# Four blocks of first products per two PSUM banks and one gelu, scores called later, left-over dots called beside the weights

## The chip, the cores and the metric

One core of a Trainium2 chip runs the kernel. The metric is the device time in microseconds (us) of one execution; the time before is the median of three runs.

## The reference, cut to what matters

The layer has two mixers (a linear recurrence and a gated linear attention) and then PEER, a channel mixer that picks experts by product keys. The change lies in PEER. For each of 512 tokens with normed vector `u` (1024 numbers), eight heads each choose 16 of 16384 experts, and the layer adds the chosen experts' outputs:

```python
q = (u @ w_q).reshape(tokens, 8 heads, 2 halves, 128)
s = einsum("thjd,hjkd->thjk", q, keys)          # 128 keys for each half
# top 16 of each half, then top 16 of the 16 x 16 sums: 16 experts per head
w = softmax(top16_scores)                       # per head
y = sum over heads and picks of  w * gelu(u . expert_u[e]) * expert_v[e]
```

## The kernel before, in words

The 512 tokens are four tiles of 128. For tiles t0 and t1 (`GT`) the kernel gathers rows of the two expert tables by an indirect DMA on the GpSimd queue (POOL): for a tile and a pick k, one gather fetches 128 rows of 4 KB (0.524 MB). For tiles d0 and d1 (`DT`) it computes all 16384 experts densely, in 128 blocks of 128 experts. A block of the first table (`ut_s`, 0.524 MB, loaded by SyncE, SP) gives the first products of both tiles, and a block of the second (`vt_s`, as large) is multiplied by the gated weights.

Four stages matter here, with their times in the profiled execution:

- **First products** (about 409 to 950 us). TensorE (PE) does 128 blocks, `d_scores` (L985 to L994): eight F32 matmuls of 128x256 per block; two blocks share one PSUM bank (`pds2`), and ScalarE (ACT) takes one gelu per bank (L994). Between the first blocks stand the eight heads' queries of the dense tiles, `q_mm` (L727, matmuls L732, copy of the result by ACT L734), and their scores, `s_mm` (L737, matmuls L742, copies L746). VectorE (DVE) picks the top 16 (`select`, L753 to L844, with an exp on ACT at L832) and, between its steps, computes dots of gathered rows of the first table (`u_row`: gather L888, dot L895), 16 at a time finished by a small gelu on ACT and a product on DVE (`u_done`, L897). `turn` (L871) transposes a dense tile's picks: DVE writes `est` (L842 and L877), PE transposes it into `ptr` (L880). `turn_i` (L902) and `turn_a` (L909) do the same for the indices (`ixf`, `pti`, `ix`) and the activations (`pta`) of t0.
- **Weights** (950 to 1142 us). 32 turns of a loop of two (L1172 to L1180): `w_hot` builds one-hot matrices `ab` on DVE and ACT, `w_mm` multiplies them on PE (`pwb`, L1015), `v_load_pairs` gathers four row groups of the second table (POOL, tiles `ring` and `ring_s`), `v_pairs` (L934) multiplies them into `yv` on PE, `w_mul` (L1024) multiplies the gelus `A` by the weights on DVE.
- **Last products** (1142 to 1550 us). 128 blocks of the second table (loop L1204 to L1221): `v_split` casts a block into a high and a low part (ACT L1037, L1038; DVE L1039, L1040), `d_out` (L1052) does 12 F32R matmuls, or 8 plain F32 ones in each sixth block. Spread over these blocks runs `rest()` (L1190): the dots of t1 that are not done yet, then its 128 row groups of the second table (`v_row`, DVE L943).
- A tail of some 19 us.

The order of the first products comes from two generators, `pe_list` (L1077) and `dve_list` (L1130), merged by planned costs (what they `yield`, and `clock` at L1154). A scheduler then orders every engine's instructions by its own estimate of times. Only the weights and the last products are pinned as written (`tc.manual_schedule`), on PE, ACT and DVE. At the end of the first products 232 of the 256 dots of gathered rows are done; 24 dots of t1 are left for `rest()`.

Of the kernel before, what the change touches and what calls it, by code (L numbers as in the profile page):

```python
# [20 lines left out]
D = 1024  # L21
# [9 lines left out]
TOPK = 16  # L31
# [16 lines left out]
def tile_kernel(ctx, tc, x, cx, pos, ada_w, cols, rows, consts, w_in, wgate, w_g, w_out, w_q, keys_t,  # L48
# [11 lines left out]
    def bank(name="ps"):  # L60
        return psum.tile([128, 512], F32, name=name, tag="ps")
# [829 lines left out]

    def u_row(t, k):
        more = "sel" not in done and k % 3 == 2
        g = gather(peer_u, sel_i[t][:, k:k + 1], zs.tile([128, D], F32, name="rz", bufs=2) if more else ring())
        V.scalar_tensor_tensor(g, g, 1.0, u_n[t], op0=OP.mult, op1=OP.mult, accum_out=act[t][:, k:k + 1])  # L895

    def u_done(t, h):  # L897
# [87 lines left out]
    def d_scores(b):  # L985
        ut = ld.pop(b)
        if b % 2 == 0:
            ld["ps"] = bank("pds2")
        p = ld["ps"][:, b % 2 * 256:b % 2 * 256 + 256]
        for k in range(KD):  # L990
            PE.matmul(p, ut[:, k], u_d[k // 4][:, k % 4].rearrange("p j t -> p (j t)"),  # L991
                      start=(k == 0), stop=(k == KD - 1))
        if b % 2:
            S.activation(a_of(b - 1, 2), ld["ps"], AF.Gelu)  # L994

# [64 lines left out]
    def u_next(t):  # L1060
# [3 lines left out]
        left[t]["u"].pop(0)  # L1064
        u_row(t, k)
        if k % TOPK == TOPK - 1:
            u_done(t, k // TOPK)
            if k == NSEL - 1 and t == t0:
                turn_a(t0)
        return True  # L1070

    def row_u():
        return u_next(t0) or (not left[t0]["u"] and u_next(t1))

    done = set()

    def pe_list():  # L1077
# [30 lines left out]
        for n, (kind, b) in enumerate(seq):  # L1108
            if n + 3 < len(seq):
                u_load(*seq[n + 3])  # L1110
            if kind == "w":
                if b % 2:
                    last = q_mm(DT, b // 2)
                    yield 7.
                continue
# [4 lines left out]
            d_scores(b)  # L1120
            if last:
                s_mm(*last)
                last = None
                yield 1.1
            yield 3.5
# [42 lines left out]
    wb = [(t, n0) for t in DT for n0 in range(0, 128, 4)]  # L1168
    with tc.manual_schedule(engines=PIN):
        gz = v_load_pairs(0, 1)  # L1170
        hot = [w_hot(*wb[n]) for n in range(2)]
        for n in range(0, 64, 2):  # L1172
# [6 lines left out]
            for q in p:  # L1179
                w_mul(*q)  # L1180
    for b in range(4):
        v_load(b)
# [7 lines left out]
    def rest():  # L1190
        for h in range(NH):
            while len(left[t1]["u"]) > NSEL - (h + 1) * TOPK:
                u_next(t1)
                yield
# [98 lines left out]
```

## Time and profile before

| | us |
|---|---|
| median of three runs | 1569.45 |
| lowest, highest | 1563.09, 1569.67 |
| profiled execution, own time | 1570.65 |
| its span in the trace | 1568.8 |
| PE busy | 1468.1 (94%) |
| DVE busy | 1191.9 (76%) |
| POOL busy | 653.5 (42%) |
| ACT busy | 533.2 (34%) |

The shares are averages over stages with different limits, so what a stage is worth must be read from that stage. Busy time of PE is what the trace models for pipelined matmuls. The profiled execution lies 1.20 us above the median. Over the span the kernel moves 484.30 MB.

### The profile page before, as it was taken

How to read it: one execution, taken by the hardware profiler on the slowest of the kernel's cores; microseconds unless marked ns; L12 is line 12 of the kernel's file. 1: busy time of each engine (PE TensorE's matmuls, PEld its weight loads, DVE VectorE, ACT ScalarE, POOL GpSimd, SP SyncE). 2: the span in 40 equal slices, each digit the busy share in tenths (PEclk: the TensorE clock that was granted, in tenths of full speed). 3: DMA queues.
4: the chain of work that ended last, by engine and by line, in shares of the span. 5: the costliest groups of instructions: out<-in, count | busy, mean ns of one | idle time of the engine just before them, and what ended most of it. 6: DMA issues, size and time to landing. Idle time of an engine off the chain costs nothing.

```text
span 1568.8 us, 20348 instructions
## 1 busy us (share of the span) xinstructions
PE 1468.1 (94%) x6668; PEld 1099.7 (70%) x6668; DVE 1191.9 (76%) x2942; ACT 533.2 (34%) x1033; POOL 653.5 (42%) x651
## 2 busy tenths in 40 slices
PE   7899999999999959998999999999979899999995
PEld 2678778468888748887888886555556676666663
DVE  5889975427999999986555545666669898988987
ACT  3657874112211211210110004455433333434333
POOL 0111100004556456475444435666535555544540
PEclk9999999999999979999999999999999999999998
DMA  9655531627899979999999998999999999999995
GB/s 372 194 185 178 160 94 54 255 85 284 309 382 331 331 259 360 346 368 351 373 377 361 389 365 279 353 354 349 345 330 367 346 393 384 379 384 363 382 369 208
DMA packets 152570, 484.30 MB, mean 309 GB/s; under 512 B 14864, under 2 KB 36752, under 8 KB 152336
## 3 DMA queue, kind: packets, MB, share of 16 engines
q0 software_dynamic: 79072, 287.87, 50.2%
q1 hardware_dynamic: 73392, 195.13, 33.5%
q8 instruction: 53, 0.87, 0.2%
q14 instruction: 53, 0.43, 0.1%
HBM read 477.69 MB, written 5.24 MB: 308 GB/s over the span
## 4 chain that ended last, share of the span: by engine, by line
PE 38%; DVE 26%; DMA 16%; issue 10%; POOL 4%; ACT 4%; DVEq 0%; POOLq 0%; ACTq 0%; SPq 0%
PE pds L991 14%; DMA ring<-in_dram,sel_i 11%; PE yv L934 7%; DVE ring L895 6%; PE pwb L1015 4%; PE pw L687 4%; POOL ring L888 3%; DVE rz L895 3%; PE ya L1052 2%; DMA rz<-in_dram,sel_i 2%; PE pq L732 1%; DVE y L943 1%; DMA wada<-in_dram 1%; DMA adw<-in_dram 1%; DVE vl L1040 1%
## 5 line engine op out<-in xcount | busy, mean ns | idle before, releaser
L888 POOL DMA_INDIRECT ring<-in_dram,sel_i x334 | 403.3, 1207 | 404.6 <-DVE ring L895 150.1
L991 PE MATMUL pds<-u_d,ut_s 128*128 128x256 f32 x2048 | 450.7, 382 | 5.0 <-DVE ix L907 5.0
L991 PEld LDWEIGHTS pds<-u_d,ut_s 128*128 128x128 f32 x2048 | 391.8, 192 | 59.1 <-DVE ix L907 5.4
L895 DVE SCALAR_TENSOR_TENSOR ring<-ring,u_n 128x1024 f32<-128x1024 f32 x206 | 255.7, 1246 | 102.1 <-DMA ring<-in_dram,sel_i 100.6
L943 DVE SCALAR_TENSOR_TENSOR y<-ring,act,y 128x1024 f32<-128x1024 f32 x127 | 162.6, 1280 | 37.2 <-DMA ring<-in_dram,sel_i 36.3
L1052 PE MATMUL ya<-vl,gh 128*128 128x512 f32 x428 | 139.3, 407 | 24.9 <-DVE vl L1040 24.6
L1052 PE MATMUL ya<-vh,gh 128*128 128x512 f32 x428 | 142.6, 415 | 2.6 <-ACT vh L1038 2.6
L1040 DVE TENSOR_TENSOR vl<-vt_s,vh 128x1024 fp32r<-128x1024 f32 x107 | 132.8, 1241 | 4.1 <-ACT vh L1038 4.1
L1052 PE MATMUL ya<-vh,gl 128*128 128x512 f32 x428 | 133.9, 394 | 0.0
L1038 ACT CAST vh<-vt_s 128x1024 fp32r<-128x1024 f32 x107 | 112.4, 1050 | 51.1 <-DMA vt_s<-in_dram 44.4
L934 PE MATMUL yv<-ring_s,z 128*64 128x512 f32 x256 | 120.5, 602 | 2.6 <-DMA ring_s<-in_dram,ix 2.5
L934 PE MATMUL yv<-ring,z 128*64 128x512 f32 x256 | 117.4, 599 | 0.0
L1052 PEld LDWEIGHTS ya<-vl,gh 128*128 128x128 f32 x428 | 78.3, 190 | 54.9 <-DVE vl L1040 39.4
L994 ACT ACTIVATE A<-pds 128x512 f32<-128x512 f32 x64 | 37.4, 596 | 225.7 <-PE pds L991 214.7
L1037 ACT CAST gh<-A 128x256 fp32r<-128x256 f32 x107 | 43.4, 406 | 191.2 <-PE ya L1052 176.8
L1000 DVE TENSOR_TENSOR ab<-cst,sel_t 128x512 f32<-128x512 f32 x64 | 44.1, 689 | 81.0 <-PE pwb L1015 50.5
L1052 PEld LDWEIGHTS ya<-vh,gh 128*128 128x128 f32 x428 | 80.7, 189 | 30.9 <-issue 9.8
L1052 PEld LDWEIGHTS ya<-vh,gl 128*128 128x128 f32 x428 | 81.0, 189 | 19.7
L888 POOL DMA_INDIRECT ring<-in_dram,ix x64 | 62.7, 980 | 50.8 <-PE yv L934 22.2
L1015 PEld LDWEIGHTS pwb<-ab 128*128 128x128 f32 x512 | 60.2, 191 | 26.4 <-issue 14.8
L1052 PE MATMUL ya<-vt_s,A 128*128 128x512 f32 x168 | 75.5, 592 | 0.0
L888 POOL DMA_INDIRECT ring_s<-in_dram,ix x64 | 61.1, 955 | 33.6 <-issue 13.5
(307 smaller groups left out, 2291.1 us busy)
## 6 DMA issues: line engine op xcount, KB each, us to landing
ut_s<-in_dram SPq DMA_DIRECT2D x144, 512.0 KB
vt_s<-in_dram SPq DMA_DIRECT2D x128, 512.0 KB
adw<-in_dram POOLq DMA_DIRECT2D x34, 512.0 KB
wraw<-in_dram SPq DMA_DIRECT2D x21, 512.0 KB
wada<-in_dram SPq DMA_DIRECT2D x16, 512.0 KB
wq<-in_dram SPq DMA_DIRECT2D x16, 512.0 KB
ring<-in_dram,sel_i POOLq DMA_INDIRECT x334
wo<-in_dram SPq DMA_DIRECT2D x8, 512.0 KB
```

The lines of the kernel that those rows point to most:

```text
L687: PE.matmul(p, mix_k(k)[:, t * 128:(t + 1) * 128], wo[k][:, n * 512:(n + 1) * 512], start=(k == 0), stop=(k == KD - 1))
L888: G.indirect_dma_start(out=g, out_offset=None, in_=tab, in_offset=bass.IndirectOffsetOnAxis(ap=ix, axis=0))
L895: V.scalar_tensor_tensor(g, g, 1.0, u_n[t], op0=OP.mult, op1=OP.mult, accum_out=act[t][:, k:k + 1])
L934: PE.matmul(yv[0][h * 64:h * 64 + 64, n, :], z[:, 63 - i:127 - i], g[:, n * 512:(n + 1) * 512], start=(i == 0), stop=(i == 63), skip_group ...
L943: V.scalar_tensor_tensor(L["y"], g, a, L["y"], op0=OP.mult, op1=OP.add)
L991: PE.matmul(p, ut[:, k], u_d[k // 4][:, k % 4].rearrange("p j t -> p (j t)"), start=(k == 0), stop=(k == KD - 1))
L1000: V.tensor_tensor(ab[:, 0], iota[:, None, :].to_broadcast([128, 4, 128]), st[0][:, j, n0:n0 + 4, None].to_broadcast([128, 4, 128]), op=OP. ...
L1015: PE.matmul(p[:, n * 128:(n + 1) * 128], ab[:, 1, n], ab[:, 0, n], start=True, stop=True)
L1037: S.copy(gh, a)
L1038: S.copy(vh, vt)
L1040: V.tensor_sub(vl, vt, vh.bitcast(F32))
L1052: PE.matmul(ya[t][:, n, :], g[:, j * 128:(j + 1) * 128], v[:, n * 512:(n + 1) * 512], start=(b == 0 and i == 0), stop=(b == 127 and i == l ...
```

## The change

Three edits. Four blocks of first products go into two neighbouring PSUM banks (`pds4`) and one gelu of 128x1024 reads them. In `pe_list` the scores of a head are called just before the queries of the next head, with a planned cost of 8.1 in place of 7 and 1.1 (the last head's after block 34). `u_row` is split into `u_start` (the gather) and `u_fin` (the dot and what follows it), and the weights loop calls them from its second turn on: the dot of the row that was started one turn earlier, then the gather of the next, into a tile `rw` that reuses the two buffers of `u_d`. `rest()` keeps what is then left.

```diff
--- before.py
+++ after.py
@@ -889,10 +889,21 @@
                              in_offset=bass.IndirectOffsetOnAxis(ap=ix, axis=0))
         return g
 
-    def u_row(t, k):
-        more = "sel" not in done and k % 3 == 2
-        g = gather(peer_u, sel_i[t][:, k:k + 1], zs.tile([128, D], F32, name="rz", bufs=2) if more else ring())
+    def u_start(t, k):
+        if "u" in done:
+            g = B.tile([128, D], F32, name="rw", tag="u_d", bufs=2)
+        elif "sel" not in done and k % 3 == 2:
+            g = zs.tile([128, D], F32, name="rz", bufs=2)
+        else:
+            g = ring()
+        return t, k, gather(peer_u, sel_i[t][:, k:k + 1], g)
+
+    def u_fin(t, k, g):
         V.scalar_tensor_tensor(g, g, 1.0, u_n[t], op0=OP.mult, op1=OP.mult, accum_out=act[t][:, k:k + 1])
+        if k % TOPK == TOPK - 1:
+            u_done(t, k // TOPK)
+            if k == NSEL - 1 and t == t0:
+                turn_a(t0)
 
     def u_done(t, h):
         a = act[t][:, h * TOPK:(h + 1) * TOPK]
@@ -984,14 +995,14 @@
 
     def d_scores(b):
         ut = ld.pop(b)
-        if b % 2 == 0:
-            ld["ps"] = bank("pds2")
-        p = ld["ps"][:, b % 2 * 256:b % 2 * 256 + 256]
+        if b % 4 == 0:
+            ld["ps"] = bank2("pds4")
+        p = ld["ps"][:, b % 4 // 2, b % 2 * 256:b % 2 * 256 + 256]
         for k in range(KD):
             PE.matmul(p, ut[:, k], u_d[k // 4][:, k % 4].rearrange("p j t -> p (j t)"),
                       start=(k == 0), stop=(k == KD - 1))
-        if b % 2:
-            S.activation(a_of(b - 1, 2), ld["ps"], AF.Gelu)
+        if b % 4 == 3:
+            S.activation(a_of(b - 3, 4), ld["ps"].rearrange("p h n -> p (h n)"), AF.Gelu)
 
     def w_hot(t, n0):
         j = DT.index(t)
@@ -1062,15 +1073,13 @@
         if k >= NSEL or k >= ready_h[t] * TOPK:
             return False
         left[t]["u"].pop(0)
-        u_row(t, k)
-        if k % TOPK == TOPK - 1:
-            u_done(t, k // TOPK)
-            if k == NSEL - 1 and t == t0:
-                turn_a(t0)
-        return True
+        return u_start(t, k)
 
     def row_u():
-        return u_next(t0) or (not left[t0]["u"] and u_next(t1))
+        g = u_next(t0) or (not left[t0]["u"] and u_next(t1))
+        if g:
+            u_fin(*g)
+        return g
 
     done = set()
 
@@ -1110,18 +1119,19 @@
                 u_load(*seq[n + 3])
             if kind == "w":
                 if b % 2:
+                    if last:
+                        s_mm(*last)
                     last = q_mm(DT, b // 2)
-                    yield 7.
+                    yield 8.1
                 continue
             if b == A1:
                 while "sel" not in done:
                     yield None
                 open_l2()
             d_scores(b)
-            if last:
+            if last and b == 34:
                 s_mm(*last)
                 last = None
-                yield 1.1
             yield 3.5
             if b == 121:
                 done.add("end")
@@ -1167,6 +1177,7 @@
     PIN = {ET.Activation, ET.PE, ET.DVE}
     wb = [(t, n0) for t in DT for n0 in range(0, 128, 4)]
     with tc.manual_schedule(engines=PIN):
+        late = []
         gz = v_load_pairs(0, 1)
         hot = [w_hot(*wb[n]) for n in range(2)]
         for n in range(0, 64, 2):
@@ -1178,6 +1189,12 @@
             gz = gzn
             for q in p:
                 w_mul(*q)
+            if 2 <= n:
+                if late:
+                    u_fin(*late.pop())
+                g = n < 56 and u_next(t1)
+                if g:
+                    late.append(g)
     for b in range(4):
         v_load(b)
     if "usage" in globals():
@@ -1190,7 +1207,7 @@
     def rest():
         for h in range(NH):
             while len(left[t1]["u"]) > NSEL - (h + 1) * TOPK:
-                u_next(t1)
+                u_fin(*u_next(t1))
                 yield
             for _ in range(TOPK):
                 v_row(t1, left[t1]["v"].pop(0))
```

The order in which each engine receives its instructions, at three places. First ACT among the first products, where the dense heads' queries are copied (`q`), the exponentials of a selection are taken (`sw`), scores are copied (`s`) and gelus of first products go to `A1`. Before:

```order
L994 ACTIVATE A1_3042<-pds2_3925 128x512
L832 ACT_TABLE_LOAD
L832 ACTIVATE sw_4497<-sw_4497 128x64
L734 COPY q_3998<-pq_3981 128x512
L899 ACT_TABLE_LOAD
L899 ACTIVATE act0_2314<-act0_2314 128x16
L746 COPY s_3751<-pss_4045 128x256
L746 COPY s_3753<-pss_4045 128x256
L994 ACTIVATE A1_3042<-pds2_4036 128x512
```

and in the changed kernel:

```order
L1005 ACTIVATE A1_3042<-pds4_3772 128x1024
L734 COPY q_3985<-pq_3968 128x512
L832 ACT_TABLE_LOAD
L832 ACTIVATE sw_4475<-sw_4475 128x64
L910 ACT_TABLE_LOAD
L910 ACTIVATE act0_2314<-act0_2314 128x16
L746 COPY s_3817<-pss_4108 128x256
L746 COPY s_3819<-pss_4108 128x256
L1005 ACTIVATE A1_3042<-pds4_3906 128x1024
```

The copy of the queries stood behind the exponential and now stands ahead of it.

Second PE, where the picks of d0 are transposed (`ptr`). Before (63 blocks of first products stand ahead of `ptr`):

```order
L991 MATMUL pds_4858<-u_d,ut_s 128x256 x16
L991 MATMUL pds_4903<-u_d,ut_s 128x256 x8
L906 MATMUL pti<-cst,ixf 128x128
L880 MATMUL ptr<-cst,est 128x128 x3
L991 MATMUL pds_4903<-u_d,ut_s 128x256 x8
L991 MATMUL pds_4965<-u_d,ut_s 128x256 x16
```

and in the changed kernel, from the last head's scores on (31 blocks stand ahead of `pti`, 43 ahead of `ptr`):

```order
L742 MATMUL pss<-kt,q 128x128 x4
L917 MATMUL pti<-cst,ixf 128x128
L1002 MATMUL pds_4068<-u_d,ut_s 128x256 x8
L1002 MATMUL pds_4204<-u_d,ut_s 128x256 x32
L1002 MATMUL pds_4290<-u_d,ut_s 128x256 x32
L1002 MATMUL pds_4393<-u_d,ut_s 128x256 x24
L880 MATMUL ptr<-cst,est 128x128 x3
L1002 MATMUL pds_4393<-u_d,ut_s 128x256 x8
```

`ptr` moved 20 blocks nearer to the start, and eight matmuls stand for one block. In both kernels the scores of a dense head still stand about one block behind its queries on PE, as in this piece of the changed kernel:

```order
L732 MATMUL pq<-u_d,ut_s 128x256 x16
L1002 MATMUL pds_3906<-u_d,ut_s 128x256 x8
L742 MATMUL pss<-kt,q 128x128 x4
L1002 MATMUL pds_3906<-u_d,ut_s 128x256 x8
L1002 MATMUL pds_4068<-u_d,ut_s 128x256 x16
```

Third DVE in the weights loop of the changed kernel, one turn:

```order
L902 SCALAR_TENSOR_TENSOR rw,act_2315<-rw,u_n_2771 128x1024
L1011 TENSOR_TENSOR ab<-cst,sel_t 128x512
L1019 TENSOR_SCALAR ab<-cst,sel_t 128x128 x3
L1011 TENSOR_TENSOR ab<-cst,sel_t 128x512
L1019 TENSOR_SCALAR ab<-cst,sel_t 128x128 x2
L1035 TENSOR_TENSOR A_3042<-A_3042,pwb 128x88x4
L1035 TENSOR_TENSOR A_5554<-A_5554,pwb 128x40x4
```

The first row is new; there are 24 such turns. On POOL each such turn has five gathers in place of four, the new one (`rw`) behind the four of the second table, and the run of gathers at the end of the queue falls from 152 to 128.

## Rows read from the trace of the kernel before

**Rows 1.** Windows: start:end, length, busy PE PEld DVE ACT POOL (count), PEclk, DMA, GB/s

```profile
409.00:610.00 201.00, 178.53 (x837) 157.02 (x837) 199.45 (x872) 32.52 (x60) 116.70 (x114) 0.94 0.90 328
950.00:1142.00 192.00, 188.96 (x1016) 97.76 (x1014) 121.92 (x343) 93.08 (x307) 117.27 (x121) 1.00 0.94 342
1160.00:1545.00 385.00, 362.46 (x1390) 257.87 (x1389) 338.29 (x383) 149.45 (x207) 191.13 (x148) 1.00 0.98 373
```

**Rows 2.** Timeline of PE among the first products: start, length, what [idle before, releaser]

```profile
580.43 2.08 PE L742 MATMUL pss<-kt,q 128*128 128x128 f32 x8 [18.96 <-ACT q L734]
...
604.93 1.05 PE L742 MATMUL pss<-kt,q 128*128 128x128 f32 x8
...
716.44 0.49 PE L880 MATMUL ptr<-cst,est 128*128 128x128 f32 x3
...
732.27 26.43 PE L991 MATMUL pds<-u_d,ut_s 128*128 128x256 f32 x112 [4.98 <-DVE ix L907]
...
807.33 138.30 PE L991 MATMUL pds<-u_d,ut_s 128*128 128x256 f32 x640
...
950.79 0.64 PE L934 MATMUL yv<-ring,z 128*64 128x512 f32 x1
```

**Rows 3.** Timeline of ACT, same columns

```profile
578.36 1.28 ACT L832 ACT_TABLE_LOAD   x1 [26.61 <-DVE sw L831]
...
579.81 0.57 ACT L734 COPY q<-pq 128x512 f32<-128x512 f32 x1
...
697.27 0.21 ACT L899 ACTIVATE act<-act 128x16 f32<-128x16 f32 x1 [16.63 <-DVE ring L895]
```

**Rows 4.** Waits of PE, 409 to 950 us: us in total, times, longest

```profile
PE pss L742 <- ACT q L734: 22.5, 2, 19.0
```

**Rows 5.** Timeline of DVE where the picks of d0 become ready

```profile
655.39 1.20 DVE L842 TENSOR_REDUCE est<-eq 128x64 f32<-128x1024 f32 x1
```

**Rows 6.** Windows just behind the two stalls

```profile
580.00:584.00 4.00, 3.57 (x12) 3.22 (x13) 4.00 (x19) 2.51 (x5) 1.87 (x2) 0.50 0.91 316
584.00:590.00 6.00, 6.00 (x24) 5.10 (x23) 6.00 (x41) 0.60 (x1) 2.81 (x3) 0.82 0.75 251
732.00:736.00 4.00, 3.73 (x9) 3.01 (x10) 4.00 (x8) 0.00 (x0) 0.03 (x1) 0.50 0.92 368
```

**Rows 7.** Groups of ACT, 409 to 950 us: busy, mean ns of one | idle before

```profile
L994 ACT ACTIVATE A<-pds 128x512 f32<-128x512 f32 x63 | 36.8, 596 | 223.2 <-PE pds L991 212.2 <-issue 11.0
```

**Rows 8.** Group of PE over the span: busy, mean ns of one | idle before

```profile
L991 PE MATMUL pds<-u_d,ut_s 128*128 128x256 f32 x2048 | 450.7, 382 | 5.0 <-DVE ix L907 5.0
```

**Rows 9.** Chain of waits in the weights stage: start, length, what

```profile
950.86 3.58 PE yv L934 x16
954.45 1.98 PE pwb L1015 x16
...
1023.44 7.79 DMA ring_s<-in_dram,ix
```

**Rows 10.** Groups of POOL: 745 to 925 us, 955 to 1135 us, 1160 to 1545 us

```profile
L888 POOL DMA_INDIRECT ring<-in_dram,sel_i x78 | 78.9, 1012 | 101.0 <-DVE ring L895 98.6 <-issue 2.1 <-DVE ab L1008 0.3
...
L888 POOL DMA_INDIRECT ring<-in_dram,ix x59 | 58.1, 984 | 45.0 <-PE yv L934 20.4 <-PE pwb L1015 16.2 <-issue 6.7
...
L888 POOL DMA_INDIRECT ring<-in_dram,sel_i x148 | 192.0, 1297 | 183.1 <-DVE y L943 132.0 <-DVE ring L895 30.5 <-DMA ring<-in_dram,sel_i 9.8
```

**Rows 11.** Timeline of POOL in the weights stage

```profile
1022.09 0.94 POOL L888 DMA_INDIRECT ring<-in_dram,ix  x1 [0.30 <-issue]
```

**Rows 12.** Waits of DVE, 950 to 1142 us

```profile
DVE ab L1000 <- PE pwb L1015: 36.3, 19, 3.5
```

**Rows 13.** Groups of DVE in the last products, 1142 to 1550 us

```profile
L943 DVE SCALAR_TENSOR_TENSOR y<-ring,act,y 128x1024 f32<-128x1024 f32 x127 | 162.6, 1280 | 37.2 <-DMA ring<-in_dram,sel_i 36.3
...
L895 DVE SCALAR_TENSOR_TENSOR ring<-ring,u_n 128x1024 f32<-128x1024 f32 x24 | 28.9, 1217 | 5.8 <-DMA ring<-in_dram,sel_i 5.8
```

**Rows 14.** Waits of PE, 1142 to 1550 us

```profile
PE ya L1052 <- DVE vl L1040: 24.6, 30, 3.2
```

## Prediction

> **What bounds the kernel now.** I read four views, stage by stage. The windows by stage come first [rows 1]. In the first products PE is busy 178.53 of 201 us up to 610 us, and DVE 199.45 of 201: there DVE is the fuller engine. In the weights PE is busy 188.96 of 192 us while the DMA engines are 94% busy. In the last products DMA is 98% busy at 373 GB/s, and PE 362.46 of 385 us. So PE and the transfers lie close together in each stage, and a gain on the one is soon stopped by the other.
>
> Second, PE's timeline through the first products [rows 2] is to be read for gaps. Two stand out: 18.96 us in front of the scores at 580.43, released by ACT's copy of the queries, and 4.98 us at 732.27, released by DVE's `ix`. Third, ACT's timeline [rows 3] says why the first is so long. The copy of the queries (579.81) waits for nothing of its own: it is behind an exponential, whose input DVE gives at 578.36 only. PE's waits for such copies sum to 22.5 us in two places [rows 4]. A gap has a second price: in the stretches behind the two, PE's granted clock was 0.50, that is its 1.2 GHz level, for 4 us each, after PE had been idle, then 0.82 in the mean [rows 6], so some 3 us more are lost behind a gap.
>
> Fourth, the chain of waits in the weights [rows 9]: 3.58 us of `yv` and 1.98 us of `pwb` per turn, 5.56 us, against 192 / 32 = 6.0 us measured; the rest is waits for gathers, one of them 7.79 us long.
>
> **Part one, gelus of four blocks.** 64 gelus of 596 ns [rows 7] become 32 of about twice the elements. They lie beside PE; their idle time is almost all waiting for PE. If a gelu stood late, PE would meet it at the second pair of banks, four blocks or 14 us on. I cost this at nothing.
>
> **Part two, the scores.** The source calls them four blocks later, but the order shows them on PE still one block behind the queries in most heads, because the scheduler puts them where it finds room. What does change is ACT: the copy of the queries now stands ahead of the exponential. That takes away the 18.96 us, and most of the 22.5 us. The next head's copy stands behind that exponential instead, but its queries are done near the time when the exponential's input comes; I allow some 7 us in small waits there.
>
> Then comes what the merged order does next. Before, the last scores start at 604.93 [rows 2], with 31 blocks done. Take off 22.5 us of waits and 3 us of slow clock, and add the 7 us: about 588 us. The new order puts the transposes of d0's picks, `ptr`, after 43 blocks where 63 stood ahead of it. A block takes 138.30 us / 40 = 3.456 us: the trace shows 2048 records for 128 blocks [rows 8], so the 640 records of the long run are 40 blocks [rows 2]. Twelve blocks more make 41.5 us, so PE is at `ptr` at about 629.5 us (622 to 632 with the allowance at its ends). Its input `est` is reduced on DVE at 655.39 plus 1.20 = 656.6 us [rows 5]. DVE was full on the way there (199.45 of 201 us), its list of selections and dots up to that point is nearly the same (109 dots for 110), and earlier scores can't fill it more. So **PE waits some 27 us at `ptr`**, more than at the gap that went. Before, the same transposes at 716.44 waited for nothing.
>
> From there: 656.6, 85 blocks at 3.456 = 293.8 us, 3 us of slow clock, about 1 us of transposes, and two pairs of `pwb` that now stand among the blocks, 2 us: 956.4. `pta` needs the dots of t0, whose last gelu came at 697.27 [rows 3]; PE gets there 13 blocks behind `ptr`, near 705, so it should pass, and the 4.98 us for `ix` goes as well, since `pti` now stands 12 blocks earlier than `ptr`. I allow 0 to 5 us for what stands late here. First `yv` at 956 to 962 in place of 950.79: **+8 us**, with -5 (DVE reaches `est` 13 us sooner) and +14 as the ends.
>
> **Part three, the dots.** 24 gathers of 0.524 MB, 12.6 MB in all, and 24 dots move from the last products to the weights. In the weights DVE has room: it waits 36.3 us for `pwb` alone [rows 12], and 24 dots of 1.217 us [rows 13] are 29 us. The queue of POOL takes five gathers per turn, 5 x (0.98 + 0.30) = 6.4 us [rows 10, 11], where the turn now takes 6.0. The transfers are the tighter: 342 GB/s at a share of 0.94 is 364 GB/s when full, so 12.6 MB are 34.6 us, of which the idle 6% of 192 us, 11.5 us, can take a part. All of that idle used gives +23, none of it +35. I take **+28 us**. The ends: 65.7 MB that the stage moves now and 12.6 MB at the last stage's 373 GB/s would be 210 us, +18; at 342 GB/s 12.6 MB are +37. What is queued behind: each new gather stands on POOL behind four of the second table, and its buffer is free only when the dot of two turns ago is done, so a late dot holds up the next turn's four gathers.
>
> In the last products 12.6 MB fewer are 33.7 us at 373 GB/s, and DVE loses 29 us of dots. But PE was idle only 385 - 362.46 = 22.5 us there, and 24.6 us of its waits are for DVE's low parts [rows 14], some of which stay. So PE becomes the bound before the saving is used up: **-20 us**, with -14 (a third of PE's idle time stays, since low parts still queue behind 127 sums of 1.28 us [rows 13]) and -27 as the ends.
>
> **The sum** against the profiled execution, 1570.65: +8 + 28 - 20 = +16, so 1586.7. That execution is 1.20 us above the median, so about **1585** by the median, 1569.45.
>
> **Rivals.** *Full gain in the middle (faster).* If `est` were ready when PE comes to `ptr`, the first `yv` would be near 927 (629.5 + 293.8 + some 4), -24, and the sum -16: 1553. The whole change comes out even if `est` is ready by 641 us. For it: with the heads' scores 20 us earlier DVE might start d0's second selection earlier, at the cost of dots that nobody waits for yet. Against it: DVE's order keeps those dots between the steps, and it was full.
>
> *Zero sum.* If transfers bound both stages fully, +34.6 and -33.7 cancel and the middle's +8 is left: 1578. For it are the shares of 0.94 and 0.98 [rows 1]; against it PE's 22.5 us of idle time, too few to take the saving.
>
> *POOL becomes the bound of the weights.* In the last products, where DVE is busy 338 of 385 us, a gather took 1297 ns on POOL, in place of 984 in the weights [rows 10]. If the dot beside them brings that to the loop, a turn is 5 x (1.30 + 0.30) = 8.0 us, 24 turns cost 24 x 2.0 = +48, and the sum is +36: 1605. It decides from where POOL's five gathers take more than the transfers' 7.2 us per turn. Against it: gathers beside dots alone, 745 to 925 us, took 1012 ns, as good as none. The Trainium skill, page "SBUF — State Buffer", section "SBUF: two separate sides", speaks for this case: a VectorE operation with two SBUF inputs and a GpSimd one that reads SBUF shut each other out for the whole instruction. By that rule one gather per turn would wait for a whole dot, a turn would take 6.4 + 1.2 = 7.6 us and the sum would be about 1595; the 1012 ns beside dots show at most a few per cent of that.
>
> That the change doesn't do what it says is already in the forecast for the scores; that all of it then stays as it was in the middle would give +8 us (28 - 20), 1577.
>
> **How the numbers follow.** Half a per cent, some 8 us, is about what a measurement of this kernel can tell from no change; so faster is below 1561.6 and slower above 1577.3. The forecast has 0.45, with its own range 1572 to 1597; the full gain 0.22; zero sum 0.15; POOL as the bound 0.13; the middle unchanged 0.05. Faster: most of the full gain and a little of the last, 0.21. Same: the lower end of the forecast 0.10, half of zero sum 0.07, and 0.06 of the full gain and the last: 0.23. Slower: 0.56. The range 1552 to 1600 leaves out nearly half of the full gain (0.1) and the upper half of POOL's case (0.08).
>
> **What would show it.** Right: on PE one wait of 20 to 30 us in front of `ptr` near 630 us and none of 19 us for a copy of the queries; weights longer by some 28 us, with PE's share of them down to 85% and turns near 7.1 us; last products near 388 us with PE's idle time mostly gone. Wrong: `ptr` without a wait, `est` ready before 641; weights that stay below +18, which would say that the DMA had more room than its share tells; gathers on POOL above 1.2 us in the weights; or a last stage that falls by under 14 us.

## The result and the profile after

The changed kernel takes 1580.19 us (median of nine, 1576.76 to 1585.68) against 1568.85 us for the kernel before (nine, 1562.46 to 1574.21): a ratio of 1.0082, interval [1.0059, 1.0104]. It is slower. The profiled execution has a span of 1581.0 us, 12.2 more than before.

Where these 12.2 us are can be read from four marks on PE: the first full turn of the weights, the first and the last matmul of the last products, and the end.

| stage | before | after | difference | forecast |
|---|---|---|---|---|
| first full turn of the weights | 950.8 | 962.7 | +11.9 | +8 |
| weights, to the first `ya` of the last products (1142.4; 1184.8) | 191.6 | 222.1 | +30.5 | +28 |
| last products (to 1550.4; 1563.7) | 408.0 | 378.9 | -29.1 | -20 |
| tail | 18.4 | 17.3 | -1.1 | 0 |

PE's timeline of the changed kernel (start, length, what, idle time before and its releaser) answers to [rows 2]:

```profile
586.79 1.67 PE L742 MATMUL pss<-kt,q 128*128 128x128 f32 x8 [3.83 <-ACT q L734]
...
588.47 42.70 PE L1002 MATMUL pds<-u_d,ut_s 128*128 128x256 f32 x192
653.43 0.69 PE L880 MATMUL ptr<-cst,est 128*128 128x128 f32 x2 [22.26 <-DVE est L877]
657.15 0.47 PE L880 MATMUL ptr<-cst,est 128*128 128x128 f32 x1 [3.03 <-DVE est L842]
...
958.01 1.07 PE L945 MATMUL yv<-ring,z 128*64 128x512 f32 x2
...
962.67 0.64 PE L945 MATMUL yv<-ring_s,z 128*64 128x512 f32 x1
```

The wait of 18.96 us for the copy of the queries has become one of 3.83, and PE is done with the last head at 588, 18 us sooner. Then it meets `ptr` at 631.2 (588.47 + 42.70) and stands for 22.26 and, for the third transpose, 3.03 us, until DVE's `est` is there. At the end two products `yv` stand ahead of the last block, so the first full turn of the weights is taken to start at 962.67. The waits of PE from 409 to 950 us (us in total, times, longest) show that nothing else is large, and that no wait for `ix` is left:

```profile
PE ptr L880 <- DVE est L877: 22.3, 1, 22.3
PE pss L742 <- ACT q L734: 7.0, 3, 3.8
PE pta L922 <- DVE act L911: 3.8, 1, 3.8
PE ptr L880 <- DVE est L842: 3.0, 1, 3.0
```

The windows by stage answer to [rows 1] (same columns):

```profile
409.00:610.00 201.00, 193.97 (x917) 170.47 (x916) 196.79 (x879) 31.47 (x54) 115.44 (x113) 0.98 0.93 338
...
962.00:1184.00 222.00, 207.44 (x1010) 100.73 (x1008) 149.29 (x389) 93.09 (x305) 149.10 (x145) 0.96 0.96 352
1184.00:1563.00 379.00, 372.02 (x1450) 273.84 (x1451) 328.70 (x366) 159.24 (x224) 175.06 (x128) 0.99 0.97 362
```

Up to 610 us PE does more (193.97 us busy for 178.53). In the weights the transfers stay at a share of 0.96 for 222 us, and PE is busy 93% of it, where it was 98%. PE's busy time rose there from 188.96 to 207.44 us for as many matmuls, at a granted clock of 0.96 in the mean, where it was 1.00 before. In the last products PE has only 7 us of idle time left in 379 us, and its waits for DVE's low parts are down from 24.6 us [rows 14] to this, over 1160 to 1565 us:

```profile
PE ya L1063 <- DVE vl L1051: 6.2, 7, 3.6
```

### The profile page after: what moved, and what is told of

Read it like the earlier page. It is cut to its first block, busy times and chain, and to the rows that moved or that the text cites. A ratio compares the mean times of both kernels' runs of the same rounds, so it can differ in the third digit from the quotient of the medians.

```text
span 1581.0 us, 20280 instructions
## 1 busy us (share of the span) xinstructions
PE 1480.3 (94%) x6668; PEld 1104.8 (70%) x6668; DVE 1190.9 (75%) x2942; ACT 527.9 (33%) x999; POOL 658.9 (42%) x651
## 4 chain that ended last, share of the span: by engine, by line
PE 51%; DVE 23%; DMA 13%; issue 7%; ACT 4%; POOL 2%; DVEq 0%; POOLq 0%; ACTq 0%; SPq 0%
PE pds L1002 16%; PE ya L1063 14%; PE yv L945 6%; DVE ring L902 6%; PE pw L687 3%; DMA ring<-in_dram,sel_i 3%; DVE rz L902 3%; PE pwb L1026 3%; DMA adw<-in_dram 2%; DMA ring_s<-in_dram,ix 2%; DMA vt_s<-in_dram 2%; PE pq L732 1%; POOL ring L888 1%; DMA wada<-in_dram 1%; DVE ti L772 1%
## 5 line engine op out<-in xcount | busy, mean ns | idle before, releaser
L888 POOL DMA_INDIRECT ring<-in_dram,sel_i x310 | 371.4, 1198 | 420.6 <-DVE y L954 155.6
L902 DVE SCALAR_TENSOR_TENSOR ring<-ring,u_n 128x1024 f32<-128x1024 f32 x182 | 227.8, 1258 | 89.4 <-DMA ring<-in_dram,sel_i 88.2
L945 PE MATMUL yv<-ring_s,z 128*64 128x512 f32 x256 | 125.9, 626 | 5.6 <-DMA ring_s<-in_dram,ix 2.9
L945 PE MATMUL yv<-ring,z 128*64 128x512 f32 x256 | 126.7, 627 | 1.1 <-DMA ring<-in_dram,ix 0.9
L1005 ACT ACTIVATE A<-pds 128x1024 f32<-128x1024 f32 x32 | 32.8, 1024 | 246.1 <-PE pds L1002 243.8
L888 POOL DMA_INDIRECT ring<-in_dram,ix x64 | 67.1, 1048 | 41.9 <-PE pwb L1026 16.4
L1026 PE MATMUL pwb<-ab 128*128 128x128 f32 x512 | 71.2, 289 | 7.7 <-ACT ab L1017 4.8
```

The lines of the kernel that those rows point to most:

```text
L888: G.indirect_dma_start(out=g, out_offset=None, in_=tab, in_offset=bass.IndirectOffsetOnAxis(ap=ix, axis=0))
L945: PE.matmul(yv[0][h * 64:h * 64 + 64, n, :], z[:, 63 - i:127 - i], g[:, n * 512:(n + 1) * 512], start=(i == 0), stop=(i == 63), skip_group ...
L1026: PE.matmul(p[:, n * 128:(n + 1) * 128], ab[:, 1, n], ab[:, 0, n], start=True, stop=True)
```

## The experiments

They ran on three chips, in three groups of four, each with the kernel before beside it: 1571.44 us with the first group, 1555.92 with the second, 1558.21 with the third. So every ratio is against before on the same chip, and stages of profiles are compared within a group where that can be done. Which chip gave the result is not on record; its stages agree with those of the first group (weights with the dots 222.1 us, and 222.9 in `a_rot`), so it is counted with the first chip here. Theory A is that of the prediction; B to G are named as they came up.

### Group 1: which edit moves the middle, and do the dots cancel

**The gelus alone** (`p_gelu`): before, with `d_scores` of the change.

```diff
-        if b % 2 == 0:
-            ld["ps"] = bank("pds2")
+        if b % 4 == 0:
+            ld["ps"] = bank2("pds4")
...
-        if b % 2:
-            S.activation(a_of(b - 1, 2), ld["ps"], AF.Gelu)
+        if b % 4 == 3:
+            S.activation(a_of(b - 3, 4), ld["ps"].rearrange("p h n -> p (h n)"), AF.Gelu)
```

> The kernel before with the four-block gelus alone; scores and left-over dots as before. Theory A (the wait at the transposes of d0's picks makes the middle longer, and it comes from the gelus' own pair of banks; the moved dots cancel between two stages): PE waits 22 to 28 us at ptr near 650 us although nothing was done to the scores, first yv near 958 to 963, and the time is 10 to 13 us above before, about 1580. Rival B (the lost time is the gathers in the weights, the middle is no worse): without the moved dots the time is at or below before, 1545 to 1570.

Measured: 1582.13 us, ratio 1.0069 [1.0047, 1.0090]. Waits of PE, 409 to 965 us:

```profile
PE ptr L880 <- DVE est L877: 24.3, 1, 24.3
PE pss L742 <- ACT q L734: 6.0, 2, 3.0
PE pta L911 <- DVE act L900: 4.4, 1, 4.4
PE ptr L880 <- DVE est L842: 3.0, 1, 3.0
```

They are the waits of the whole change. So the edit of the gelus alone takes the 19 us wait away and brings the one at `ptr`; the edit of the scores isn't needed for either. B falls: without a moved dot the kernel is as slow. A reason can be read from the source: before, blocks of first products and transposes share one rotation of four banks, and `ptr` gets its bank in its turn, after 63 blocks. With the blocks in pairs of banks of their own, a single bank is free early, and the scheduler puts `ptr` after 43. The run `a_rot` below tests this.

**The change without the dots** (`a_nodots`): the six lines in the weights loop and the tile `rw` taken out.

```diff
...
-            if 2 <= n:
-                if late:
-                    u_fin(*late.pop())
-                g = n < 56 and u_next(t1)
-                if g:
-                    late.append(g)
```

> The changed kernel with the 24 left-over dots put back into the last products. Theory A: weights back to 190 to 195 us, last products back to 405 to 410, so +30.5 and -29.1 us vanish together and the time stays at 1578 to 1580. Rival B: the weights give back more than the last products take, 1550 to 1560.

Measured: 1582.63 us, ratio 1.0081 [1.0056, 1.0107], that of the whole change. The group of `yv` on `ring_s` (duration min/median/max, first and last start) and the first matmul of the last products:

```profile
L943 PE MATMUL yv<-ring_s,z x256: 592/592/644, 961.3 to 1153.0; 128*64 128x512 f32 x128
```

```profile
1154.19 0.73 PE L1061 MATMUL ya<-vh,gh 128*128 128x512 f32 x2 [0.61 <-ACT vh L1047]
```

The weights are back to 192.9 us (961.3 to 1154.2), the last products, to 1561.2, back to 407. On this chip the moved dots cancel.

**Transposes back in the rotation** (`a_rot`, `a_rot_nodots`): the change, with

```diff
-        p = bank("ptr")
+        p = bank2("ptr")[:, 0]
...
-        p = bank("pti")
+        p = bank2("pti")[:, 0]
...
-        p = bank("pta")
+        p = bank2("pta")[:, 0]
...
-        p = bank("pwb")
+        if t == d0 and n0 < 8:
+            if n0 == 0:
+                ld["pwb"] = bank2("pwb")
+            p = ld["pwb"][:, n0 // 4]
+        else:
+            p = bank("pwb")
```

> The changed kernel, but the transposes of picks, indices and activations and the first two pairs of weights take their banks from the same rotation as the four-block gelus, so that PE meets ptr after 61 blocks in place of 43, pta after 73 and the second ptr after 85. Theory A: no wait at ptr, some 1.5 us for each of the five tiles that now take a pair of banks, first yv at 930 to 942 in place of 958 to 963, time 1550 to 1560, 9 to 19 us below before. Rival C (transfers bound the middle too): PE waits for ut_s loads instead of est, first yv not before 948, time 1565 or more.

> The same with the 24 dots back in the last products. Theory A (dots cancel): within 5 us of the run with the dots beside the weights, 1550 to 1560. Rival B: 25 to 30 us faster than it.

Measured: 1579.75 us, 1.0055 [1.0037, 1.0074], and 1583.57 us, 1.0079 [1.0047, 1.0110]. The expected gain did not come. PE's waits in the first of the two, 409 to 965 us:

```profile
PE pds L1002 <- ACT A L1005: 17.1, 3, 13.6
PE ptr L880 <- DVE ix L918: 10.6, 1, 10.6
PE pss L742 <- ACT q L734: 6.8, 2, 3.8
```

The wait for `est` is gone and `ptr` stands after 61 blocks, which shows that the banks had moved it. Two others took its place, as large: gelus that stand on ACT behind an exponential whose input DVE gives later, and `ptr`, now behind `pti` in the same rotation, which waits for DVE's `ix`. ACT's timeline has the first:

```profile
656.02 1.28 ACT L832 ACT_TABLE_LOAD   x1 [23.77 <-DVE sw L831]
...
658.88 1.02 ACT L1005 ACTIVATE A<-pds 128x1024 f32<-128x1024 f32 x1
```

A gelu whose blocks were done on PE at 632 us starts at 658.88, behind an exponential for whose input ACT waited 23.77 us. PE runs ahead of DVE's selections here, and whatever of DVE stands next in a queue in front of PE's work takes the gain. The two runs without and with the dots lie within 4 us of each other, so the dots cancel again.

### Group 2: the parts alone, ACT's order mended, rows without their bytes

**The dots alone** (`p_dots`): before, with `u_start`, `u_fin` and the weights loop of the change.

> The kernel before with the left-over dots in the weights alone. Theory A (the dots' cost in the weights, +30, and their saving in the last products, -29, cancel): within 4 us of before, first yv unchanged near 951, weights 218 to 226 us, last products 376 to 384. Rival B (the slower time of the whole change comes from here): 8 us or more above before.

Measured: 1549.35 us, ratio 0.9963 [0.9947, 0.9978], 6.6 us below before, where theory A allowed 4. Windows of the weights and the last products:

```profile
951.00:1150.00 199.00, 197.19 (x1008) 97.15 (x1004) 151.23 (x393) 97.55 (x308) 143.17 (x144) 1.00 1.01 392
1150.00:1529.00 379.00, 371.93 (x1450) 273.97 (x1451) 329.35 (x367) 159.09 (x224) 168.01 (x128) 0.99 0.97 363
```

The first `yv` is where it was (950.8). By their marks the weights take 200 us, where the next two runs, same chip, no dots there, take 180 and 179: +20 to +21, not +30, while the last products fall nearly as before, from 405 and 403 to 379. On this chip the dots are a small gain. The stage is shorter here without the dots too: 180 us, where `a_nodots` on the first chip takes 193.

**The scores alone** (`p_scores`): before, with `s_mm` called ahead of the next `q_mm`.

```diff
                 if b % 2:
+                    if last:
+                        s_mm(*last)
                     last = q_mm(DT, b // 2)
-                    yield 7.
+                    yield 8.1
...
-            if last:
+            if last and b == 34:
                 s_mm(*last)
                 last = None
-                yield 1.1
```

> The kernel before with the scores called four blocks later alone. Theory A (the scheduler orders PE and ACT as before, the copy of the queries still stands behind the exponential): the 19 us wait for the copy stays, and the time is within 3 us of before. Rival D (the later call is what took the 19 us wait away): that wait is gone and the time is 15 to 25 us below before.

Measured: 1553.22 us, 0.9982 [0.9959, 1.0005]. Neither expectation holds whole. PE's waits, 409 to 965 us:

```profile
PE pds L991 <- ACT A L994: 12.0, 3, 6.2
PE pds L991 <- DVE ix L907: 7.4, 1, 7.4
PE pss L742 <- ACT q L734: 3.5, 1, 3.5
```

The 19 us wait went: in this kernel the scores do stand later on PE (three blocks between queries and scores at 564.74 us of the trace, where the changed kernel has one). But gelus behind exponentials and `ix` hold PE up for about as long, and the time stays.

**ACT's order mended** (`b_fix`): before, with each exponential of the dense tiles, and each small gelu from the sixth on, tied to a block by a bias of zero made from that block's gelu (blocks 39, 47 and 53 for the exponentials; for the first of them from the seventh head's queries), and `pti` in a free pair of banks.

```diff
-        S.activation(sv, sv, AF.Exp)
+        if t in DT and EXP_AFTER[t - d0, h0] is not None:
+            zc = kb.tile([128, 1], F32, name="zc", bufs=2)
+            src = EXP_AFTER[t - d0, h0]
+            S.activation(zc, held[src] if src < 0 else a_of(src)[:, 0:1], AF.Copy, scale=0.0)
+            S.activation(sv, sv, AF.Exp, bias=zc)
...
-        S.activation(a, a, AF.Gelu)
...
+            S.activation(zc, a_of(min(b, held["last"]))[:, 0:1], AF.Copy, scale=0.0)
+            S.activation(a, a, AF.Gelu, bias=zc)
...
-        p = bank("pti")
+        p = bank2("pti")[:, 0]
```

> The kernel before, with ACT's exponentials and small gelus of the dense stage tied to blocks that PE has reached by the time their input is there (a bias of zero taken from that block), and the indices of t0 transposed into a bank of the unused pairs. Theory A (PE's waits in the middle come from ACT's queue order and shared banks, and there is nothing else to bound it): the 19 us and 5 us waits go and none takes their place, first yv at 922 to 932 in place of 951, time 20 to 28 us below before. Rival C (the transfers bound the middle once PE doesn't wait): PE waits for ut_s, first yv at 940 or later, gain under 12 us. Rival E (PE meets the next late input of DVE instead, as in the run with shared banks): one wait of 10 us or more on PE for another releaser, gain under 12 us.

Measured: 1544.71 us, ratio 0.9938 [0.9917, 0.9959], 11 us below before. The waits of PE, and its timeline:

```profile
PE pta L929 <- DVE act L918: 13.4, 1, 13.4
PE pti L924 <- DVE ixf L922: 5.7, 1, 5.7
```

```profile
587.55 110.67 PE L1009 MATMUL pds<-u_d,ut_s 128*128 128x256 f32 x512
698.06 0.49 PE L891 MATMUL ptr<-cst,est 128*128 128x128 f32 x3
...
746.51 0.45 PE L929 MATMUL pta<-cst,act 128*128 128x128 f32 x1 [13.42 <-DVE act L918]
...
941.09 0.64 PE L952 MATMUL yv<-ring,z 128*64 128x512 f32 x1
```

The waits for `q`, `ix`, `est` and gelus are all gone; which of the ties took which away, this run doesn't part. What E named came true, one wait of over 10 us and a gain of under 12. Its cause is the edit itself: the last small gelu of t0 was tied too late, and with an earlier tie (`best`, below) the wait for `act` is gone. First `yv` at 941, 10 us sooner, and the time follows it.

**Rows without their bytes** (`a_narrow`): the change, whose gathers beside the weights fetch 64 numbers a row (those 24 dots are then other numbers).

```diff
...
+            g4 = kb.tile([128, 64], F32, name="rn", bufs=2)
+            return t, k, (g, gather(peer_u.rearrange("e (c d) -> (e c) d", d=64), sel_i[t][:, k:k + 1], g4))
...
+        if type(g) is tuple:
+            V.scalar_tensor_tensor(g[0], u_n[t], g[1][:, 0:1], u_n[t], op0=OP.mult, op1=OP.mult,
+                                   accum_out=act[t][:, k:k + 1])
```

> The changed kernel; the 24 gathers beside the weights fetch 64 numbers per row in place of 1024, and their dots run as long as before over another tile, so POOL's and DVE's instructions stay and the 12.6 MB go (those 24 dots are not the reference's). Theory A (transfers set the weights' time): weights at 192 to 200 us in place of 222, time 20 to 28 us below the changed kernel, 1552 to 1562. Rival F (POOL's fifth gather, or the dot on DVE, sets it): weights stay at 214 us or more, time above 1572.

Measured: 1565.51 us, 1.0059 [1.0041, 1.0076]. Without the 12.6 MB the weights still take 206 us (961.6 to 1167.6), 6 more than with whole rows on that chip (`p_dots`). That lies between what A and F expected. Window and POOL's groups, 975 to 1140 us:

```profile
975.00:1140.00 165.00, 159.81 (x794) 78.94 (x792) 125.76 (x321) 78.62 (x247) 128.41 (x121) 1.00 0.91 317
```

```profile
L888 POOL DMA_INDIRECT ring_s<-in_dram,ix x49 | 52.2, 1065 | 14.9 <-issue 9.8 <-PE pwb L1032 2.7 <-PE yv L951 1.2
L888 POOL DMA_INDIRECT ring<-in_dram,ix x50 | 49.4, 987 | 15.8 <-PE pwb L1032 6.7 <-issue 5.2 <-PE yv L951 2.7
L888 POOL DMA_INDIRECT rn<-in_dram,sel_i x22 | 27.3, 1242 | 6.7 <-issue 5.2 <-DMA ring<-in_dram,ix 1.2 <-DMA ring_s<-in_dram,ix 0.3
```

So transfers don't set these 206 us. DMA is down to 0.91, and POOL has no gap: 121 gathers of 1.06 us and 37.4 us of pauses, 0.31 each, are 165.8 of 165 us. That is theory F: five gathers a turn fill POOL's queue, with few bytes too. One thing makes this run dearer than whole rows. The mean of 1242 ns is of two kinds: nine of the 22 narrow gathers begin while no dot runs and take 0.95 us, and the other 13 begin in a running dot and take 1.44 us in the mean (see group 3). Over the stage all gathers lose 13 us in this way. An estimate without it: five times 0.94 + 0.30 is 6.2 us, still more than PE's 5.56 per turn, so 24 turns would cost 15 of the 20 us that the dots cost on this chip.

### Group 3: gather or dot, and a version to beat both

**The changed kernel again** (`again`).

> The changed kernel once more, on the chip of the next three, as their measure. 5 to 16 us above before. After the run with narrow rows, theory A's part on the weights (transfers set their time) is in doubt; theory F (five gathers per turn on POOL, each with its pause) says that POOL is without a gap in the weights, busy time plus 0.30 us for each gather filling 95% or more of it; theory A says that DMA is at 0.96 or more and POOL waits for PE.

Measured: 1560.24 us, 1.0016 [0.9996, 1.0036]: on this chip the change costs nothing that can be measured, below the 5 us that were the least expected. The middle is the same (a wait of 21.0 and one of 3.0 at `ptr`, first `yv` of the full turn at 958.6), the last products too (379), but the weights take 198.6 us and not 222. Window and POOL's groups, 970 to 1130 us:

```profile
970.00:1130.00 160.00, 158.94 (x799) 77.31 (x796) 126.69 (x325) 79.37 (x252) 122.07 (x124) 1.00 1.02 403
```

```profile
L888 POOL DMA_INDIRECT ring<-in_dram,ix x51 | 51.7, 1015 | 16.0 <-issue 7.0 <-PE pwb L1026 6.1 <-PE yv L945 2.9
L888 POOL DMA_INDIRECT ring_s<-in_dram,ix x51 | 50.5, 990 | 15.6 <-issue 8.2 <-PE pwb L1026 7.0 <-PE yv L945 0.3
L888 POOL DMA_INDIRECT rw<-in_dram,sel_i x22 | 21.1, 959 | 6.7 <-issue 6.4 <-DVE ab L1019 0.3
```

Here too POOL is full (122.07 us and 38.3 of pauses in 160), and the transfers with it, at 403 GB/s, so this run can't part the two. On the first chip they moved 352 GB/s in this stage at a share of 0.96, and POOL's groups, 970 to 1175 us, had 62.2 us of idle time with 143.8 busy, more than the 43 us that 139 pauses make: there POOL waited for PE to free its buffers, up to 2.3 us at a time. That the slower transfers are behind it is argued.

**Dots without gathers** (`a_nogather`) and **gathers without dots** (`a_nodot`), each the change with the other half left out of the weights loop (24 dots run over a resident tile; or are missing in the output).

> The changed kernel without the 24 gathers beside the weights; their dots run as long over a resident tile (those 24 dots are not the reference's). Theories A and F: weights fall by 18 us or more against the changed kernel of the same chip. Theory G (the dot on DVE holds up the one-hot matrices): they fall by less than 6.

> The changed kernel with the 24 gathers beside the weights but without their dots (which the output then lacks). Theories A and F: weights within 6 us of the changed kernel of the same chip. Theory G: they fall by 18 us or more. If a dot beside a gather lengthens it, the mean of a gather in the weights falls from 1.0 to 1.07 us to 0.95 or less, and the weights by 5 x 0.08 us per turn, 8 to 12 us in all.

Measured: 1540.51 us, 0.9881 [0.9850, 0.9911], and 1557.56 us, 0.9995 [0.9978, 1.0013]. Windows of the weights, of the one and of the other:

```profile
961.00:1144.00 183.00, 182.97 (x1008) 95.87 (x1006) 147.78 (x388) 96.36 (x305) 129.94 (x121) 1.00 0.97 360
```

```profile
962.00:1160.00 198.00, 196.30 (x1008) 96.17 (x1006) 120.87 (x342) 98.06 (x305) 139.29 (x145) 1.00 1.01 394
```

By the marks the weights take 183.0 and 198.2 us, against 198.6 in `again`. So taking out the gathers gains 16 us, a little less than A and F expected, and taking out the dots gains nothing; G falls. One thing was against expectation: POOL's gathers with resident dots beside them,

```profile
L888 POOL DMA_INDIRECT ring_s<-in_dram,ix x56 | 67.3, 1202 | 17.4 <-issue 10.1 <-PE yv L946 5.5 <-PE pwb L1027 1.8
L888 POOL DMA_INDIRECT ring<-in_dram,ix x56 | 54.1, 967 | 21.9 <-PE pwb L1027 8.5 <-PE yv L946 7.0 <-issue 6.4
```

take 1202 ns in one of the two groups and 967 in the other. The timelines of POOL and DVE say why:

```profile
980.42 0.94 POOL L888 DMA_INDIRECT ring<-in_dram,ix  x1 [0.30 <-issue]
981.07 1.22 DVE L902 SCALAR_TENSOR_TENSOR rw<-u_n 128x1024 f32<-128x1024 f32 x1
981.67 1.43 POOL L888 DMA_INDIRECT ring_s<-in_dram,ix  x1 [0.30 <-PE yv L946]
```

The first gather was under way when the dot began, and takes 0.94 us. The second begins in the running dot and ends at 983.10, 0.81 us behind the dot's end. All 24 gathers of this stage that begin in a dot, all of them `ring_s`, end 0.80 to 0.82 us behind its end and take 1.17 to 1.74 us; those in which a dot begins take 0.93 or 0.94. The Trainium skill, page "SBUF — State Buffer", section "SBUF: two separate sides", has a VectorE operation with two SBUF inputs and a GpSimd one that reads SBUF shut each other out. The trace agrees for the gather, which waits for the rest of the dot that it begins in; the dots keep their 1.22 us. What it costs is then a matter of when gathers begin: in `a_nogather` it adds 12 us to POOL over the stage (24 gathers of 1.46 us in place of 0.94), in `again` 3 us, since there most gathers that begin in a dot do so near its end. So the means there are 984 ns with dots and 970 without.

**A version to beat both** (`best`): `b_fix` with the last small gelu of t0 tied to block 59 in place of 65, and one left-over dot at every second turn of the weights.

```diff
...
-            if 2 <= n:
+            if True:
...
-                g = n < 56 and u_next(t1)
+                g = n % 4 == 0 and n < 62 and u_next(t1)
```

> The kernel before with the queue order of the run that tied ACT's exponentials and small gelus to blocks (the last small gelu of t0 tied earlier, so that PE doesn't wait for it), and one left-over dot beside every second turn of the weights, 16 in all, 8 left to the last products. Theory A for the middle: no wait over 4 us on PE among the first products, first yv at 924 to 934. Theory F for the weights: nine gathers in two turns take 9 x 1.27 = 11.4 us on POOL against PE's 11.1, so the weights are at most 6 us longer than without dots, and the last products 16 to 20 us shorter. Together 24 to 36 us below before. Theory C (transfers bound the middle) or A in the weights: 12 to 20 us below.

Measured: 1559.46 us, 1.0003 [0.9982, 1.0023]. The gain that was expected didn't come. The middle did nearly what was expected: no wait of PE in it above 4.6 us, blocks done and both first pairs of weights through at 926. Then PE waited for the first gathered rows. PE's wait, the gather of these rows on POOL, and the transfers at that time:

```profile
931.17 1.94 PE L963 MATMUL yv<-ring,z 128*64 128x512 f32 x2 [5.11 <-DMA ring<-in_dram,ix]
925.47 0.94 POOL L899 DMA_INDIRECT ring<-in_dram,ix  x1 [0.97 <-DVE ring L913]
920.00:930.00 10.00, 6.06 (x36) 5.36 (x34) 6.07 (x11) 3.17 (x7) 5.47 (x6) 1.00 0.82 277
```

The weights and the last products:

```profile
926.00:1130.00 204.00, 193.01 (x1011) 97.58 (x1010) 146.16 (x388) 98.47 (x308) 144.93 (x144) 0.97 1.00 388
1130.00:1544.00 414.00, 384.40 (x1450) 277.84 (x1450) 337.24 (x383) 159.80 (x225) 183.18 (x136) 0.96 0.91 340
```

PE was ready before the first rows of the weights had landed. Their gather began at 925.47 only, when a dot on DVE had freed its buffer, and the transfers, at a share of 1.00 from 880 to 920 us, were down to 0.82 as PE waited. So what held PE up at that point is DVE's last dots and not full transfers; whether full transfers had made these dots late, as theory C would have it, isn't shown. And the last products took 414 us with the transfers at 0.91 only. In it the eight dots left go through `rw`, whose two buffers are those of the low parts `vl`; DVE waited 28.8 us for them, in seven waits, and PE 25.6 us for `vl`. That is the likeliest reason for the longer stage; whether eight dots in `ring` would have kept the middle's gain wasn't tried. Of the versions that do all of the layer's work, `b_fix` (0.9938) and `p_dots` (0.9963) are faster than the kernel before.

## Why the prediction was right, point by point

The forecast was +16 us on the profiled execution and 1585 us; measured were +12.2 and 1580.19, inside the range and of the sign that was given the most chance. The mechanism was right, a wait at `ptr` in the middle and dots that nearly cancel. That the number came so near is in part luck: the terms were off by +3.9, +2.5 and -9.1 us, which offset each other, and on the third chip the same kernel is at 1.0016, where a forecast of +16 us would have missed.

- **Middle, +8 forecast, +11.9 measured.** Each step can be found. The queries' wait is gone, small waits of 7.0 us stand in its place (7 allowed). PE reached `ptr` at 631.2 (629.5), `est` came at 657.15 (656.6), the two waits were 25.3 us (27). From there to the full turn of the weights PE took 5.7 us more than forecast: 3.83 us for `pta`, which was expected to pass, 1 us for the two `yv` that stand ahead of the last block, and some slow clock behind the wait at `pta` (0.77 in the mean from 708 to 712 us). That the wait comes from the order of PE and not from the scores is shown by the run with the gelus alone, which has all of it. What the prediction lacked is the cause of that order: it read `ptr` at 43 blocks from the order, and only the run with the rotation restored showed that the banks had put it there.
- **Weights, +28 forecast, +30.5 measured, on the first chip.** The transfers were at 0.96 there, close to what +28 needs; that they set the time there is argued, as no run on that chip isolates it. One sign was missed: PE's share was to fall to 85% and is 93%, since its busy time rose by 18.5 us. Up to 9 us of that, an estimate, are the clock (0.96 over 222 us in place of 1.00), which the forecast left out of this stage. On the second and third chip the stage moved 392 and 393 GB/s. The dots cost 20 us on the second, and the gathers alone 16 us on the third. There "the transfers are the tighter" is not shown: POOL's 6.4 us per turn, which the prediction had worked out and set aside, is what a turn took (160 us hold 25 turns by their 799 matmul records at 32 to a turn), and the run with narrow rows shows a full POOL without the bytes. The rival had the right engine and the wrong price: it took 1.30 us for a gather, measured were means of 0.96 to 1.07. Its other price, a wait for a whole dot in each turn, was too high as well: a gather waits for the rest of a dot, and only where it begins in one, which made 3 us in all in `again`.
- **Last products, -20 forecast, -29.1 measured.** This term was mis-sized, beyond its end of -27. The step that failed is "PE becomes the bound before the saving is used up", which took PE's busy time as a floor. PE's idle time fell from 27 us (408 - 380.75) to 7 us (379 - 372.0), and its busy time fell by 8.7 us as well, for the same matmuls. Most of that can be read around a wait of the kernel before:

```profile
1308.80 0.62 PE L1052 MATMUL ya<-vh,gl 128*128 128x512 f32 x2
1309.26 0.61 PE L1052 MATMUL ya<-vh,gh 128*128 128x512 f32 x2
1310.68 0.73 PE L1052 MATMUL ya<-vl,gh 128*128 128x512 f32 x2 [0.81 <-DVE vl L1040]
1311.24 0.63 PE L1052 MATMUL ya<-vh,gl 128*128 128x512 f32 x2
```

In a row without a wait a pair of matmuls starts every 0.46 us, so two pairs take 0.92. Around the wait the two pairs are busy for 0.61 and 0.56 us before the next one starts, 0.25 more. The waits for low parts fell from 30 to 7, and 23 times 0.25 are, as an estimate, 5.8 of the 8.7 us. So a wait on PE cost more than its idle time, and removing it gave both back.
- **The zero-sum rival** was the right reading of the moved dots on the first chip (+30.5 and -29.1), as `a_nodots` showed by a time that stayed. It was given a chance of 0.15 because PE's idle time seemed too small, the same error as in the last term.
- **Full gain in the middle** didn't happen, and its condition, `est` by 641, was missed by 16 us, as forecast.

That the whole change measured 1.0082 on one chip and 1.0016 on another fits the stage times: middle and last products agree within 5 us between the two profiles, and the weights differ by 23.5. Of these some 13 are there without the dots as well (193 us on the first chip, 180 on the second), so the dots cost about 10 us more on the first, which is the difference between the two ratios. For the third chip there is no profile of the stage without both. Two things stay open: why the transfers of one chip are slower, and whether a cheaper gather on POOL would shorten the weights on the other two, where the transfers are full as well; only the bytes were taken away, not POOL's price.

## What to carry to other kernels

A wait that is removed in front of an engine that runs ahead of its supplier comes back at the next thing the supplier must give; before a price is put on it, list what else on that engine and on the queues between (here ACT's exponentials, shared banks, transposes) depends on the supplier, in order of its due times. An order made by a scheduler may rest on a shared pool: giving one user its own buffers moves the others, so read the order of all of them after such a change. And busy time is no floor: it can fall with the same work, as it did here in the last products, where it held the cost of waits that went.

## What the runs showed of the hardware

A gather of 128 rows costs POOL 0.94 us and a pause of 0.3 us before the next, whether its rows have 4 KB or 256 bytes (0.95 us in `a_narrow`); its price on that queue doesn't follow the bytes. If it begins while a dot of two SBUF tiles runs on DVE, it ends 0.8 to 0.9 us behind the dot's end, in the weights of `a_nogather`, `a_narrow`, `again` and the changed kernel alike, and takes up to 1.98 us. And with the same kernel and order, the transfers of the weights stage ran at 352 GB/s on one chip and 393 GB/s on another, each at a share of 0.96 or more; the change lost 0.8% on the one and nothing that can be measured on the other.
